# Feed-forward output product of a two-layer encoder: ten of eleven column groups as seven products of halves, and two of the seven placed between the norms

## The chip, the cores and the metric

The kernel runs on one core of one Trainium2 chip. The metric is the time of one execution on the device in microseconds; the time before is the median of three runs. TensorE is called PE below, VectorE DVE, ScalarE ACT, GpSimd POOL, and SyncE, which issues most of the DMA transfers, SP.

## The reference

Two layers on 512 tokens of 1024 features, in float32. Each layer has a feed-forward block, a token mixer, an attention into 256 memory tokens, and a second feed-forward block, each followed by a layer norm:

```python
def swiglu(x, w_gate, w_up, w_down):
    return (jax.nn.silu(x @ w_gate) * (x @ w_up)) @ w_down
...
#  x <- LN(alpha*x + 0.5*SwiGLU_1(x))
#  x <- LN(alpha*x + Mixer_i(x))
#  x <- LN(alpha*x + MemCrossAttn(x, mem))
#  x <- LN(alpha*x + 0.5*SwiGLU_2(x))
```

So there are four feed-forward blocks, called FFN0 to FFN3 below in order of time; the inner width is 2816 = 11 x 256. The mixer of the first layer follows FFN0, memory attention follows that, then FFN1, FFN2, the mixer of the second layer, memory attention again and FFN3, whose norm writes the output.

## The kernel before

**Tiles.** The 512 tokens are four tiles `x[0]` to `x[3]` of 128 tokens by 1024 features, kept in SBUF all the time (named `x0` to `x3` in the rows of an order). A transposed copy, in two parts `xh` and `xl`, feeds the projections. Every float32 product is three matmuls (`mm3`): each operand is split into a high and a low part, and high x high, high x low and low x high are accumulated in one PSUM bank. PSUM has eight banks, as three rings: three banks with the tag `a`, two with `d`, three with `t`. A bank of a ring is handed to the next tile of that tag when all users of the last one are done. SBUF work tiles come from a ring of 27 called `slab`, weights are loaded into a ring of two called `raw`.

**One feed-forward block (`ffn`).** The inner 2816 columns are eleven groups of 256. `hidden` computes a group: gate and up projections of two blocks of 128 columns (96 matmuls of 128x512), and `gated` multiplies. Then comes the output product, in two forms:

- `down_fast` takes two groups at once. The 512 tokens by 512 inner rows by 1024 outputs are cut in halves, so that the product is a 2x2 product of blocks, which is done with seven products of halves instead of eight. A product has two banks (b = 0, 1) with 6 matmuls each, so a pair of groups takes 84 matmuls. The sums and differences of halves that it needs are made on DVE (`mix`). The products are numbered as in the code and run in the order 1, 6, 2, 5, 7, 3, 4. Products 2, 3 and 4 go on in the banks of 1, 5 and 7 and add to them, so a bank is first added into `x` by DVE (the eviction), then gets the next product, and is evicted again to another place. Products 1 and 6 are evicted into `u2`, a slab that collects over all pairs of a block. `u2` is owed to six quarter tiles of `x`.
- `down` is the plain form: for each token tile and each half of the outputs one bank, three matmuls for each 128 inner rows, and an eviction into `x`.

Before, pairs 0 to 3 go through `down_fast`: columns 256g and 1024+256g. Then six additions on POOL put `u2` into `x` (tensor_tensor of 128x512, from SBUF to SBUF). Groups 8, 9 and 10 are plain: `down` for group 8, and one `down` for groups 9 and 10, which also does the layer norm of each token tile as soon as its two banks are evicted, and then (`to_features`) transposes it for the next stage, or writes it out in FFN3.

**The norm.** The last evictions give row sums as they go (`st`); DVE makes the negative mean `nmu`, ACT squares with a sum, POOL makes the reciprocal root `lny` in two small steps, and DVE does two passes over the 128x1024 tile (`scalar_tensor_tensor` with `ln_g`, then with `ln_b`).

**What sets the order.** All instructions are recorded by `Graph` and then emitted in one go, each engine's in the order that a greedy list scheduler finds: of what is ready by modelled costs, the one that stands first in the program. All instructions therefore carry line 140 (`op.call()`), and are told apart by the names of their tiles. On the chip each engine runs its queue in that order, and waits at an instruction whose operands or bank aren't ready.

Of the kernel before, what the change touches and what calls it, by code (L numbers as in the profile page):

```python
# [16 lines left out]
AF = mybir.ActivationFunctionType  # L17
ALU = mybir.AluOpType
AX = mybir.AxisListType

P = 128
D = 1024
S = 512
NT = S // P
# [225 lines left out]
class Kernel:  # L250
# [167 lines left out]
        v = self.x[t][:, h * 512 : (h + 1) * 512]  # L418
        self.nc.vector.scalar_tensor_tensor(out=v, in0=ps, scalar=coef, in1=v, op0=ALU.mult, op1=ALU.add)

    def down(self, acts, wts, coef, ln=None):

        nc = self.nc
        n = len(acts)
        for t in range(NT):
            st = self.small(2, "st") if ln else None
            for h in range(2):
                ps = self.ps("d")
                for i in range(n):
                    a = [z[:, t * P : (t + 1) * P] for z in acts[i]]  # L430
                    w = [z[:, h * 512 : (h + 1) * 512] for z in wts[i]]
                    self.mm3(ps, a, w, i == 0, i == n - 1)
                v = self.x[t][:, h * 512 : (h + 1) * 512]
                acc = {"accum_out": st[:, h : h + 1]} if ln else {}
                nc.vector.scalar_tensor_tensor(out=v, in0=ps, scalar=coef, in1=v, op0=ALU.mult, op1=ALU.add, **acc)
            if ln:
                self.layer_norm(t, st, ln["gb"])
                if ln["last"]:
                    dst = self.out.rearrange("(r c) d -> c r d", c=GRID_W)[16 * t : 16 * t + 16]
                    nc.sync.dma_start(out=dst, in_=self.x[t])  # L440
                else:
                    self.to_features(t)
# [59 lines left out]
        self.split(z, hi, lo)  # L502
        return hi, lo

    def down_fast(self, h1, h2, w, r1, r2, coef, u2):

        nc = self.nc
        a11, a21, a12, a22 = h1[:, 0], h1[:, 1], h2[:, 0], h2[:, 1]  # L510
        flat = lambda z: z.rearrange("p b n -> p (b n)")
        a11, a21, a12, a22 = map(flat, (a11, a21, a12, a22))

        def mix(dst, x, y, op):
            nc.vector.tensor_tensor(out=dst, in0=x, in1=y, op=op)
            return dst

        bs = {}
        for name, r, c in (("11", r1, 0), ("12", r1, 512), ("22", r2, 512), ("21", r2, 0)):
            z = self.slab(F32, (P, 2, 512))  # L520
            nc.sync.dma_start(out=z, in_=w[r : r + 256, c : c + 512].rearrange("(b p) f -> p b f", p=P))
            bs[name] = z

        def wide(z):
            got = self.slab(F32R, (P, 2, 512)), self.slab(F32R, (P, 2, 512))
            self.split(z, *got)
            return got

        left, right = {}, {}
        left[1] = self.split_pair(a11)  # L530
        right[1] = wide(bs["11"])
        t1 = mix(self.slab(F32, (P, 2, 512)), bs["12"], bs["11"], ALU.subtract)
        t2 = mix(self.slab(F32, (P, 2, 512)), bs["22"], t1, ALU.subtract)
        t3 = mix(bs["12"], bs["22"], bs["12"], ALU.subtract)
        s1 = mix(self.t2(F32), a21, a22, ALU.add)
        s2 = mix(self.t2(F32), s1, a11, ALU.subtract)
        left[6], right[6] = self.split_pair(s2), wide(t2)
        hh, hl = wide(h2.rearrange("p s b n -> p s (b n)"))
        left[2], left[4] = (hh[:, 0], hl[:, 0]), (hh[:, 1], hl[:, 1])
        right[2] = wide(bs["21"])  # L540
        t4 = mix(bs["21"], bs["21"], t2, ALU.subtract)
        left[5], right[5] = self.split_pair(s1), wide(t1)
        s3 = mix(self.t2(F32), a11, a21, ALU.subtract)
        left[7], right[7] = self.split_pair(s3), wide(t3)
        s4 = mix(self.t2(F32), a12, s2, ALU.subtract)
        left[3], right[3] = self.split_pair(s4), wide(bs["22"])
        right[4] = wide(t4)

        x = self.x
        n1, n2 = slice(0, 512), slice(512, 1024)  # L550
        first = u2 is None
        if first:
            u2 = self.slab(F32, (P, 2, 512))
        into = {
            1: lambda b: u2[:, b], 6: lambda b: u2[:, b], 2: lambda b: x[b][:, n1], 5: lambda b: x[2 + b][:, n2],
            7: lambda b: x[2 + b][:, n2], 3: lambda b: x[b][:, n2], 4: lambda b: x[2 + b][:, n1],
        }
        banks = {}
        for m, tag in ((1, "d"), (6, "t"), (2, 1), (5, "t"), (7, "d"), (3, 5), (4, 7)):
            for b in range(2):  # L560
                ps = banks[m, b] = self.ps(tag) if isinstance(tag, str) else banks[tag, b]
                for q in range(2):
                    st = [z[:, q * 256 + b * P : q * 256 + (b + 1) * P] for z in left[m]]
                    self.mm3(
                        ps, st, [z[:, q] for z in right[m]], isinstance(tag, str) and q == 0, q == 1, skip_group_check=True
                    )
                v = into[m](b)
                if m == 1 and first:
                    nc.scalar.activation(v, ps, AF.Copy, scale=coef)
                else:  # L570
                    nc.vector.scalar_tensor_tensor(out=v, in0=ps, scalar=coef, in1=v, op0=ALU.mult, op1=ALU.add)
        return u2

    def ffn(self, i, ln_i, last, aside=None):

        nc = self.nc
        wg, wu, wd = (self.a[n][i] for n in ("ffn_w_gate", "ffn_w_up", "ffn_w_down"))
        coef, u2 = 0.5 / ALPHA, None
        for g in range(4):
            h1, h2 = (self.slab(F32, (P, 2, 2, 256)) for _ in range(2))  # L580
            if g == 0:
                self.ffn_by_tokens(wg, wu, i == 0, h1)
            else:
                self.hidden(wg, wu, 256 * g, h1)
            self.hidden(wg, wu, 1024 + 256 * g, h2)
            u2 = self.down_fast(h1, h2, wd, 256 * g, 1024 + 256 * g, coef, u2)
            if g == 0 and aside:
                nc.after = [op for op in nc.ops if op.dma][-1], {"sync"}
                aside()
                nc.after = None  # L590
        for t, h in ((0, 1), (2, 0), (2, 1), (1, 1), (3, 0), (3, 1)):
            v = self.x[t][:, h * 512 : (h + 1) * 512]
            nc.gpsimd.tensor_tensor(out=v, in0=v, in1=u2[:, t % 2], op=ALU.add)
        acts, ws = [], []
        for g in range(8, 11):
            acts += [self.split_pair(z) for z in self.hidden(wg, wu, 256 * g)]
            if g == 9:
                continue
            rows = [8] if g == 8 else [9, 10]
            gb = self.load_ln(ln_i) if g == 10 else None  # L600
            ws = [z for r in rows for z in self.w_rows(wd, 256 * r)]
            self.down(acts, ws, coef, {"gb": gb, "last": last} if g == 10 else None)
            acts = []


    def transposed(self, parts):
# [583 lines left out]
    def run(self, phases=8):  # L1190
        nc, a = self.nc, self.a
        self.ident = self.tile(self.cst, [P, P], F32, "ident")
        make_identity(self.tc.nc, self.ident)
        self.xh = self.tile(self.big, [P, KB, S], F32R, "xh")
        self.xl = self.tile(self.big, [P, KB, S], F32R, "xl")
        self.x = []
        for t in range(NT):
            self.x.append(self.tile(self.big, [P, D], F32, f"x{t}"))
        self.nhalf = self.tile(self.cst, [P, 8], F32, "nhalf")
        nc.gpsimd.memset(self.nhalf, -0.5)  # L1200
        self.junk = self.tile(self.cst, [P, D], BF16, "junk")
        steps = [
            lambda last: self.ffn(0, 0, last, self.masks),
            lambda last: self.mixer_ab(1, last),
            lambda last: self.memory(0, 2, last),
            lambda last: self.ffn(1, 3, last, self.bias_tables),
            lambda last: self.ffn(2, 4, last),
            lambda last: self.mixer_c(5, last),
            lambda last: self.memory(1, 6, last),
            lambda last: self.ffn(3, 7, last),  # L1210
        ]
        for i in range(phases):
            steps[i](i == phases - 1)
        nc.emit()
# [72 lines left out]
```

## Time and profile before

| | |
|---|---|
| Time, median of three runs | 2249.1 us (2248.18 to 2251.29) |
| Profiled execution: its time / its span | 2250.06 us / 2248.3 us |
| PE busy | 2207.0 us, 98% of the span, 11312 matmuls |
| DVE busy | 1420.1 us, 63% |
| ACT busy | 882.7 us, 39% |
| POOL busy | 287.0 us, 13% |
| Mean granted clock of TensorE | 0.996 |
| DMA | 221.09 MB, 98 GB/s over the span |

The profile is of one execution; its time is the span and 1.8 us around it, and it lies 1.0 us above the median of the three runs. A row of a group gives the engine, the operation, the tile written and the tiles read, the count, busy time and mean duration, and the idle time of that engine just before. A row of the timeline gives the start and the duration in us. DVE's consecutive instructions overlap by some 0.08 us in these rows, and the matmuls of PE too, so that the pitch from start to start says more of PE than the duration of one.

### The profile page before, as it was taken

The numbers are of one execution on the slowest core, as the hardware profiler recorded it, in microseconds if no ns is written. First come the engines' busy times: TensorE is split into PE (matmuls) and PEld (weight loads), VectorE is DVE, ScalarE is ACT, GpSimd is POOL, SyncE is SP. The second block draws the span as 40 slices with busy tenths as digits, with TensorE's granted clock in tenths as the row PEclk, the third lists the DMA queues.
The fourth block names the chain that finished last, engine by engine and source line by source line (L and its number), as shares of the span: only waits on it lengthen the run. The fifth ranks groups of instructions, "written<-read, shape, count | busy, mean of one in ns | idle before, by whom it ended". The sixth has DMA issues, their size and how long they took to land. (4 is left out here: it accounts for less than half of the span.)

```text
span 2248.3 us, 28157 instructions
## 1 busy us (share of the span) xinstructions
PE 2207.0 (98%) x11312; PEld 1871.7 (83%) x11312; DVE 1420.1 (63%) x2116; ACT 882.7 (39%) x1418; POOL 287.0 (13%) x391
## 2 busy tenths in 40 slices
PE   8999999999999999999999999999999999999998
PEld 7888888778898888888888888888888988888886
DVE  5666646788745766665655667368776457666653
ACT  4323332566433433333333333256554434333331
POOL 0000203543000100001100003013411001000011
PEclk9999999999999999999999999999999999999999
DMA  6333241003333332225312334212233333322241
GB/s 207 129 120 113 67 154 57 20 20 90 124 106 113 113 113 90 72 83 168 105 40 86 113 117 150 75 62 68 69 113 96 129 113 113 113 82 72 85 137 38
DMA packets 168755, 221.09 MB, mean 98 GB/s; under 512 B 6192, under 2 KB 136880, under 8 KB 168624
## 3 DMA queue, kind: packets, MB, share of 16 engines
q1 hardware_dynamic: 165552, 208.80, 28.9%
q0 software_dynamic: 3072, 10.49, 1.3%
q8 instruction: 89, 1.46, 0.3%
q14 instruction: 42, 0.34, 0.1%
HBM read 217.17 MB, written 4.19 MB: 98 GB/s over the span
## 5 line engine op out<-in xcount | busy, mean ns | idle before, releaser
L140 PE MATMUL a<-xh,slab 128*128 128x512 f32 (+1 forms) x2960 | 890.8, 382 | 0.0
L140 PEld LDWEIGHTS a<-xh,slab 128*128 128x128 f32 x2960 | 549.1, 188 | 107.1
L140 PE MATMUL d<-slab,slab 128*128 128x512 f32 (+2 forms) x2432 | 572.5, 384 | 4.7 <-DVE slab L140 2.8
L140 PE MATMUL a<-xl,slab 128*128 128x512 f32 (+1 forms) x1480 | 565.0, 382 | 0.0
L140 PEld LDWEIGHTS d<-slab,slab 128*128 128x128 f32 x2432 | 441.1, 188 | 94.3 <-DVE slab L140 4.2
L140 ACT CAST slab<-raw 128x1024 fp32r<-128x1024 f32 x316 | 320.7, 1050 | 310.9 <-DMA raw<-ffn_w_gate 129.8
L140 DVE TENSOR_TENSOR slab<-raw,slab 128x1024 fp32r<-128x1024 f32 x316 | 391.6, 1254 | 72.9 <-ACT slab L140 55.4
L140 PEld LDWEIGHTS a<-xl,slab 128*128 128x128 f32 x1480 | 278.3, 188 | 53.0
L140 DVE TENSOR_TENSOR slab<-slab,slab 128x1024 fp32r<-128x1024 f32 (+2 forms) x208 | 241.4, 1184 | 18.9 <-ACT slab L140 17.6
L140 ACT CAST slab<-slab 128x1024 fp32r<-128x1024 f32 (+1 forms) x144 | 140.1, 1000 | 238.4 <-DVE slab L140 238.3
L140 ACT CAST slab<-t 128x512 fp32r<-128x512 f32 (+3 forms) x261 | 143.5, 572 | 225.9 <-DVE t L140 142.0
L140 PE MATMUL a<-slab,slab 128*128 128x256 f32 (+3 forms) x1336 | 204.9, 303 | 6.2 <-DVE slab L140 2.6
L140 DVE TENSOR_TENSOR slab<-a,t 128x512 f32<-128x512 f32 x56 | 38.7, 691 | 269.3 <-PE a L140 269.3
L140 PEld LDWEIGHTS a<-slab,slab 128*128 128x128 f32 x1336 | 180.6, 194 | 21.5 <-DVE slab L140 6.0
L140 DVE TENSOR_TENSOR slab<-t,slab 128x512 fp32r<-128x512 f32 (+3 forms) x261 | 164.3, 654 | 42.7 <-ACT slab L140 41.5
L140 DVE SCALAR_TENSOR_TENSOR x<-d,x 128x512 f32<-128x512 f32 x216 | 147.3, 685 | 48.3 <-PE d L140 47.3
L140 PE MATMUL t<-slab,slab 128*128 128x512 f32 (+1 forms) x648 | 152.1, 379 | 0.0
L140 ACT ACTIVATE t<-a 128x512 f32<-128x512 f32 (+2 forms) x104 | 57.4, 552 | 225.2 <-PE a L140 203.0
L140 POOL TENSOR_TENSOR x<-x,slab 128x512 f32<-128x512 f32 x24 | 46.0, 1950 | 780.7 <-DVE x L140 780.7
L140 PEld LDWEIGHTS t<-slab,slab 128*128 128x128 f32 x648 | 115.7, 188 | 25.0 <-DVE slab L140 2.2
L140 POOL TENSOR_TENSOR t<-t,l 128x256 f32<-128x256 f32 (+2 forms) x104 | 80.1, 785 | 308.4 <-DVE l L140 308.4
L140 PE MATMUL a<-slab,xh 128*128 128x256 f32 (+1 forms) x432 | 98.1, 319 | 4.1 <-ACT xh L140 4.0
(97 smaller groups left out, 1810.0 us busy)
## 6 DMA issues: line engine op xcount, KB each, us to landing
raw<-ffn_w_gate SPq DMA_DIRECT2D x40, 1024.0 KB
raw<-ffn_w_up SPq DMA_DIRECT2D x40, 1024.0 KB
slab<-ffn_w_down SPq DMA_DIRECT2D x64, 512.0 KB
raw<-ffn_w_down SPq DMA_DIRECT2D x12, 1024.0 KB
raw<-mem_w_kv SPq DMA_DIRECT2D x8, 1024.0 KB
raw<-mem_w_kv SPq DMA_DIRECT2D x16, 512.0 KB
raw<-mem_w_q SPq DMA_DIRECT2D x8, 1024.0 KB
raw<-mem_w_o SPq DMA_DIRECT2D x8, 1024.0 KB
```

Of the source, the lines that this page charges most:

```text
L140: op.call = lambda: fn(*args, **kw)
```

## The change

`ffn` now takes five pairs through `down_fast`: columns (0, 1024), (256, 1280), (512, 1536), (768, 1792) and (2048, 2304). Only the group at 2560 stays plain. The seven products run in the order 1, 6, 2, 5, 3 and then 7, 4; the last two are handed back as a function `rest`. In pairs 0 to 3 it is called at once. In pair 4 it is called after `down`, with its norms, has dealt with token tiles 0 and 1 (products 7 and 4 go only to tiles 2 and 3), and `down` of tiles 2 and 3 follows. The six additions on POOL now stand right behind product 6 of pair 4. `down`, which the mixers and the memory attention use as well, takes its banks from `d` for the first half of the outputs and from `a` for the second.

```diff
-    def down(self, acts, wts, coef, ln=None):
+    def down(self, acts, wts, coef, ln=None, blocks=range(NT)):
...
-        for t in range(NT):
+        for t in blocks:
...
-                ps = self.ps("d")
+                ps = self.ps("da"[h])
...
-        for m, tag in ((1, "d"), (6, "t"), (2, 1), (5, "t"), (7, "d"), (3, 5), (4, 7)):
...
+        def run(*steps):
+            for m, tag in steps:
...
+                if m == 6 and last:
+                    for t, n in ((0, n2), (1, n2), (2, n1), (2, n2), (3, n1), (3, n2)):
+                        nc.gpsimd.tensor_tensor(out=x[t][:, n], in0=x[t][:, n], in1=u2[:, t % 2], op=ALU.add)
+
+        run((1, "d"), (6, "t"), (2, 1), (5, "t"), (3, 5))
+        return u2, lambda: run((7, "d"), (4, 7))
...
-        for g in range(4):
+        for g, (c1, c2) in enumerate(((0, 1024), (256, 1280), (512, 1536), (768, 1792), (2048, 2304))):
...
-        for t, h in ((0, 1), (2, 0), (2, 1), (1, 1), (3, 0), (3, 1)):
-            v = self.x[t][:, h * 512 : (h + 1) * 512]
-            nc.gpsimd.tensor_tensor(out=v, in0=v, in1=u2[:, t % 2], op=ALU.add)
-        acts, ws = [], []
-        for g in range(8, 11):
...
-            self.down(acts, ws, coef, {"gb": gb, "last": last} if g == 10 else None)
-            acts = []
+        acts = [self.split_pair(z) for z in self.hidden(wg, wu, 2560)]
+        gb = self.load_ln(ln_i)
+        ws, ln = self.w_rows(wd, 2560), {"gb": gb, "last": last}
+        self.down(acts, ws, coef, ln, range(2))
+        rest()
+        self.down(acts, ws, coef, ln, range(2, NT))
```

The first place is POOL's queue at the additions of FFN3. `slab_2922_3003` is `u2` before, `slab_2979_3060` is `u2` after the change; `x0` to `x3` are the token tiles, and a row with x2 is two instructions. Before:

```order
L140 TENSOR_TENSOR x2_6_87<-x2_6_87,slab_2922_3003 128x512
L140 TENSOR_TENSOR x3_7_88<-x3_7_88,slab_2922_3003 128x512
L140 TENSOR_TENSOR x0_4_85<-x0_4_85,slab_2922_3003 128x512
L140 TENSOR_TENSOR x1_5_86<-x1_5_86,slab_2922_3003 128x512
L140 TENSOR_TENSOR x2_6_87<-x2_6_87,slab_2922_3003 128x512
L140 TENSOR_TENSOR x3_7_88<-x3_7_88,slab_2922_3003 128x512
L140 DMA slab_3217_3298<-ln_g 128x1024
L140 DMA slab_3218_3299<-ln_b 128x1024
```

And now:

```order
L140 DMA slab_3296_3377<-ln_g 128x1024
L140 TENSOR_TENSOR x0_4_85<-x0_4_85,slab_2979_3060 128x512
L140 TENSOR_TENSOR x2_6_87<-x2_6_87,slab_2979_3060 128x512 x2
L140 TENSOR_TENSOR x1_5_86<-x1_5_86,slab_2979_3060 128x512
L140 TENSOR_TENSOR x3_7_88<-x3_7_88,slab_2979_3060 128x512 x2
L140 DMA slab_3297_3378<-ln_b 128x1024
```

The six additions are the same in kind and number. They now go by the half of `u2` that they read: three with the first half (one for x0, two for x2), then three with the second. The load of `ln_g` has moved ahead of them, that of `ln_b` stays behind them.

The second place is DVE's queue from the evictions of product 6 to those of product 3, in the last `down_fast` of FFN3. In the rows a source `d_...` or `t_...` is a bank that is evicted: `slab<-t` is product 6 into `u2`, `x0<-d` and `x1<-d` product 2, `x2<-t` and `x3<-t` product 5, `x2<-d` and `x3<-d` product 7, `x0<-t` and `x1<-t` product 3. A row `slab<-raw,slab` makes the low part of weights. Before:

```order
L140 SCALAR_TENSOR_TENSOR slab_2922_3003<-t_3145_3226,slab_2922_3003 128x512
L140 SCALAR_TENSOR_TENSOR x0_4_85<-d_3142_3223,x0_4_85 128x512
L140 TENSOR_TENSOR slab_3152_3233<-raw_3150_3231,slab_3151_3232 128x1024
L140 SCALAR_TENSOR_TENSOR x1_5_86<-d_3143_3224,x1_5_86 128x512
L140 SCALAR_TENSOR_TENSOR x2_6_87<-t_3146_3227,x2_6_87 128x512
L140 TENSOR_TENSOR slab_3154_3235<-raw_3150_3231,slab_3153_3234 128x1024
L140 SCALAR_TENSOR_TENSOR x3_7_88<-t_3147_3228,x3_7_88 128x512
L140 SCALAR_TENSOR_TENSOR x2_6_87<-d_3148_3229,x2_6_87 128x512
L140 TENSOR_TENSOR slab_3157_3238<-raw_3155_3236,slab_3156_3237 128x1024
L140 SCALAR_TENSOR_TENSOR x3_7_88<-d_3149_3230,x3_7_88 128x512
L140 SCALAR_TENSOR_TENSOR x0_4_85<-t_3146_3227,x0_4_85 128x512
```

And now:

```order
L140 SCALAR_TENSOR_TENSOR slab_2979_3060<-t_3275_3356,slab_2979_3060 128x512
L140 SCALAR_TENSOR_TENSOR x0_4_85<-d_3272_3353,x0_4_85 128x512
L140 TENSOR_TENSOR slab_3280_3361<-raw_3278_3359,slab_3279_3360 128x1024
L140 SCALAR_TENSOR_TENSOR x1_5_86<-d_3273_3354,x1_5_86 128x512
L140 TENSOR_TENSOR slab_3282_3363<-raw_3278_3359,slab_3281_3362 128x1024
L140 TENSOR_TENSOR slab_3285_3366<-raw_3283_3364,slab_3284_3365 128x1024
L140 SCALAR_TENSOR_TENSOR x2_6_87<-t_3276_3357,x2_6_87 128x512
L140 TENSOR_TENSOR slab_3287_3368<-raw_3283_3364,slab_3286_3367 128x1024
L140 SCALAR_TENSOR_TENSOR x3_7_88<-t_3277_3358,x3_7_88 128x512
L140 SCALAR_TENSOR_TENSOR x0_4_85<-t_3276_3357,x0_4_85 128x512
L140 SCALAR_TENSOR_TENSOR x1_5_86<-t_3277_3358,x1_5_86 128x512
```

The evictions of product 7 have gone from this place, those of product 3 follow those of product 5, and one more row of weights stands ahead of product 5's first eviction. That eviction, into x2, now has to come after POOL's third addition, which writes the same half of x2; product 5's second eviction, into x3, after the sixth. Before, nothing of POOL stood ahead of either. On PE, 40 matmuls now stand from the rest of product 6 (its last four matmuls for each bank, in one run) up to the first bank of product 3 and 51 up to its second; they are those of products 2 and 5 and some of the last hidden group's projection.

The third place is the end of FFN3 on DVE: the norms of the first tiles. Here `x,st<-d` or `x,st<-a` is the last eviction of a half with its row sums, `nmu` the mean, `x<-x,nmu,slab` and `x<-x,lny,slab` the two passes of the norm. Before:

```order
L140 SCALAR_TENSOR_TENSOR x0_4_85,st_3229_3310<-d_3231_3312,x0_4_85 128x512
L140 TENSOR_SCALAR nmu_3232_3313<-st_3229_3310 128x1
L140 SCALAR_TENSOR_TENSOR x0_4_85<-x0_4_85,nmu_3232_3313,slab_3217_3298 128x1024
L140 SCALAR_TENSOR_TENSOR x1_5_86,st_3235_3316<-d_3236_3317,x1_5_86 128x512
L140 SCALAR_TENSOR_TENSOR x0_4_85<-x0_4_85,lny_3234_3315,slab_3218_3299 128x1024
L140 SCALAR_TENSOR_TENSOR x1_5_86,st_3235_3316<-d_3237_3318,x1_5_86 128x512
L140 TENSOR_SCALAR nmu_3238_3319<-st_3235_3316 128x1
L140 SCALAR_TENSOR_TENSOR x1_5_86<-x1_5_86,nmu_3238_3319,slab_3217_3298 128x1024
```

And now:

```order
L140 SCALAR_TENSOR_TENSOR x0_4_85,st_3303_3384<-a_3305_3386,x0_4_85 128x512
L140 SCALAR_TENSOR_TENSOR x1_5_86,st_3309_3390<-d_3310_3391,x1_5_86 128x512
L140 TENSOR_SCALAR nmu_3306_3387<-st_3303_3384 128x1
L140 SCALAR_TENSOR_TENSOR x1_5_86,st_3309_3390<-a_3311_3392,x1_5_86 128x512
L140 TENSOR_SCALAR nmu_3312_3393<-st_3309_3390 128x1
L140 SCALAR_TENSOR_TENSOR x0_4_85<-x0_4_85,nmu_3306_3387,slab_3296_3377 128x1024
L140 SCALAR_TENSOR_TENSOR x2_6_87<-d_3315_3396,x2_6_87 128x512
L140 SCALAR_TENSOR_TENSOR x0_4_85<-x0_4_85,lny_3308_3389,slab_3297_3378 128x1024
L140 SCALAR_TENSOR_TENSOR x1_5_86<-x1_5_86,nmu_3312_3393,slab_3296_3377 128x1024
L140 SCALAR_TENSOR_TENSOR x3_7_88<-d_3316_3397,x3_7_88 128x512
L140 SCALAR_TENSOR_TENSOR x1_5_86<-x1_5_86,lny_3314_3395,slab_3297_3378 128x1024
```

The banks of tile 1 are evicted before the passes of tile 0's norm, and the evictions of product 7 (into x2 and x3, from `d`) stand between the passes of the norms of tiles 0 and 1. On PE the same stretch holds 24 matmuls of `down` for tiles 0 and 1, 24 of products 7 and 4, and 24 of `down` for tiles 2 and 3, where before it held 96 of `down` for four tiles.

More of the change, by code (lines that the diff above doesn't have):

```diff
@@ L558, in down_fast @@
         banks = {}
-        for m, tag in ((1, "d"), (6, "t"), (2, 1), (5, "t"), (7, "d"), (3, 5), (4, 7)):
[L560 to L572, printed above, removed]
+        def run(*steps):
+            for m, tag in steps:
+                for b in range(2):
+                    ps = banks[m, b] = self.ps(tag) if isinstance(tag, str) else banks[tag, b]
+                    for q in range(2):
+                        st = [z[:, q * 256 + b * P : q * 256 + (b + 1) * P] for z in left[m]]
+                        self.mm3(
+                            ps, st, [z[:, q] for z in right[m]], isinstance(tag, str) and q == 0, q == 1, skip_group_check=True
+                        )
+                    v = into[m](b)
+                    if m == 1 and first:
+                        nc.scalar.activation(v, ps, AF.Copy, scale=coef)
+                    else:
+                        nc.vector.scalar_tensor_tensor(out=v, in0=ps, scalar=coef, in1=v, op0=ALU.mult, op1=ALU.add)
+                if m == 6 and last:
[3 more added lines that the diff above has]
+        return u2, lambda: run((7, "d"), (4, 7))
     def ffn(self, i, ln_i, last, aside=None):
@@ L583, in ffn @@
             else:
-                self.hidden(wg, wu, 256 * g, h1)
-            self.hidden(wg, wu, 1024 + 256 * g, h2)
-            u2 = self.down_fast(h1, h2, wd, 256 * g, 1024 + 256 * g, coef, u2)
+                self.hidden(wg, wu, c1, h1)
+            self.hidden(wg, wu, c2, h2)
+            u2, rest = self.down_fast(h1, h2, wd, c1, c2, coef, u2, g == 4)
+            if g < 4:
+                rest()
             if g == 0 and aside:
@@ L590, in ffn @@
                 nc.after = None
-        for t, h in ((0, 1), (2, 0), (2, 1), (1, 1), (3, 0), (3, 1)):
-            v = self.x[t][:, h * 512 : (h + 1) * 512]
-            nc.gpsimd.tensor_tensor(out=v, in0=v, in1=u2[:, t % 2], op=ALU.add)
-        acts, ws = [], []
-        for g in range(8, 11):
[L596 to L601, printed above, removed]
-            self.down(acts, ws, coef, {"gb": gb, "last": last} if g == 10 else None)
-            acts = []
+        acts = [self.split_pair(z) for z in self.hidden(wg, wu, 2560)]
+        gb = self.load_ln(ln_i)
+        ws, ln = self.w_rows(wd, 2560), {"gb": gb, "last": last}
+        self.down(acts, ws, coef, ln, range(2))
+        rest()
+        self.down(acts, ws, coef, ln, range(2, NT))
     def transposed(self, parts):
```

2 lines of the change are left out of this document (1 added, 1 removed).

## The prediction

> **What bounds the kernel now.** I read the page's busy times first, then the waits of PE, then the chain that ended last, and then the timeline of one feed-forward block. Busy times:
>
> ```profile
> PE 2207.0 (98%) x11312; PEld 1871.7 (83%) x11312; DVE 1420.1 (63%) x2116; ACT 882.7 (39%) x1418; POOL 287.0 (13%) x391
> ```
>
> PE works all the time. The view of its waits (what was waited for, total us, times, longest) adds up to 29.6 us in thirteen rows; the largest are the load of the input and the end of the norms:
>
> ```profile
> PE t L140 <- DMA x<-x: 6.9, 2, 5.8
> PE a L140 <- ACT xh L140: 4.0, 1, 4.0
> PE t L140 <- DVE x L140: 3.1, 4, 1.2
> PE d L140 <- DVE slab L140: 2.8, 8, 0.7
> ```
>
> No row names POOL's additions or an eviction as what holds a product. The chain of waits runs through long unbroken stretches of PE in FFN3, and gives the price of a 128x512 matmul: 43.29 us / 191 = 0.2266 us.
>
> ```profile
> 2014.21 43.29 PE a L140 x191
> ```
>
> So a matmul taken out of a feed-forward block is worth its full 0.2266 us, and a new wait of PE costs its full length. About 0.2%, 4.5 us, is what a measurement of this kernel can tell from no change. The profiled execution took 2250.06 us, 1.0 above the median of the runs; I make the sum as a difference and put it on the median.
>
> **Part 1: fewer matmuls.** A pair of groups takes 2 x 48 = 96 matmuls in the plain form and 84 as seven products. One more pair in each of four blocks: 4 x 12 x 0.2266 = **-10.9 us**, wholly on PE's path. The sums of halves, splits and evictions that the fifth pair brings to DVE lie beside PE as those of the first four do (DVE 63%); I put them at nothing. If that cover were gone, the row of 2.8 us above (eight waits for a slab of DVE, in all blocks) shows the size.
>
> **Part 2: the additions of POOL ahead of product 3.** Before, they ran when all of the pair was evicted and plain work followed. In the timeline of FFN3 (start, duration):
>
> ```profile
> 2133.78 11.52 POOL L140 TENSOR_TENSOR x<-x,slab 128x512 f32<-128x512 f32 x6 [243.39 <-DVE x L140]
> ```
>
> The four batches take 11.50 to 11.52 us; the tile's view has the spread of the 24 (min/median/max ns):
>
> ```profile
> L140 POOL TENSOR_TENSOR x<-x,slab x24: 1281/2238/2371, 265.3 to 2144.0; 128x512 f32<-128x512 f32 x24
> ```
>
> One alone takes 1.28 us. The others are long because they alternate with DVE's weight rows, which read two operands from SBUF and are drawn out too, from 1.21 us outside to 1.99 within, while evictions from PSUM keep their 0.68:
>
> ```profile
> 2128.72 1.21 DVE L140 TENSOR_TENSOR slab<-raw,slab 128x1024 fp32r<-128x1024 f32 x1
> ...
> 2135.72 0.69 DVE L140 SCALAR_TENSOR_TENSOR x<-t,x 128x512 f32<-128x512 f32 x1 [0.29 <-PE t L140]
> 2136.33 1.99 DVE L140 TENSOR_TENSOR slab<-raw,slab 128x1024 fp32r<-128x1024 f32 x1
> 2138.24 0.68 DVE L140 SCALAR_TENSOR_TENSOR x<-t,x 128x512 f32<-128x512 f32 x1
> ```
>
> The Trainium skill, "SBUF — State Buffer", section "Who interferes with whom", says that DVE and GpSimd share a pair of ports as an exclusive lock, which an instruction of DVE takes when both inputs are in SBUF and GpSimd reads there, and not with one input in SBUF. These rows agree (1.99 against 0.68 us). The rule speaks against an early place for the additions, where four such rows of DVE wait in the same stretch.
>
> Now the additions begin when product 6 is evicted, and who waits for them? Product 5's first eviction adds into the half of x2 that the third addition writes, its second into x3 behind the sixth. Product 3 goes on in product 5's banks, so PE's first matmul of its second bank stands behind the sixth addition. All of PE's queue stands behind that matmul: the last hidden group, with nothing to go around it. The times, in the numbers of FFN3 before:
>
> ```profile
> 2124.84 2.00 PE L140 MATMUL t<-slab,slab 128*128 128x512 f32 x8
> ...
> 2126.33 0.68 DVE L140 SCALAR_TENSOR_TENSOR slab<-t,slab 128x512 f32<-128x512 f32 x1
> ```
>
> The first row is the rest of product 6; the second its first eviction, which ends at 2127.01. In the new order of PE, product 3's second bank starts 51 matmuls behind the start of that first row: 2124.84 + 51 x 0.2266 = 2136.40. Evicted it is at 2127.01 + 0.08 (the gap from engine to engine) + 11.52 + 0.08 + 0.68 = 2139.4. So PE stands still for **3.0 us** in a block, part of it (about 1) ahead of the first bank, which the third addition holds: 4 x 3.0 = **+12.0 us**. Bounds: six additions of 1.28 take 7.7 us, and the wait is gone, 0; six of 2.37 take 14.2 us, 5.7 each, +22.8. I take 11.52, since the new stretch holds four weight rows of DVE like the old one.
>
> DVE stands in order behind its eviction too, so its weight rows and the next gating come late by the same 3 us; PE is late by then as well, and I add nothing.
>
> **Part 3: the ends of the blocks.** Behind the start of the last `down`, PE had 96 matmuls and has 72 now, 24 x 0.2266 = 5.4 us less to hide the norms under; DVE has four evictions (products 7 and 4) more among them, about 4 x 0.6 = 2.4 us. Before, PE and DVE were close there. The end of FFN2, ahead of the second mixer:
>
> ```profile
> 1445.10 11.50 PE L140 MATMUL d<-slab,slab 128*128 128x512 f32 x50
> ...
> 1474.02 1.29 DVE L140 SCALAR_TENSOR_TENSOR x<-x,lny,slab 128x1024 f32<-128x1024 f32 x1 [0.38 <-POOL lny L140]
> ...
> 1475.45 1.06 PE L140 MATMUL t<-ident,x 128*128 128x128 f32 x8 [0.50 <-DVE x L140]
> ```
>
> The last tile's norm ended 30.2 us behind the first `down` matmul and PE waited 0.50 for it. DVE's own work there (per tile two evictions, two passes of 1.2 and two splits of 0.6, with the small steps 5.4 us) can't be moved up by 5.4 us: counted through in the new order, tile 2's norm is done about 24 us behind the first `down` matmul, where PE has come through its 72 matmuls (16.3), the transposes of two tiles and half a projection at 21.4. So PE waits 2.8 for tile 2 and some 1.4 more for tile 3: **+4.2**. Ahead of the first mixer and of FFN2 more projection work lies ready: I take +1.0 and +1.5 for FFN0 and FFN1. In FFN3 nothing follows; the end was
>
> ```profile
> 2215.57 21.95 PE L140 MATMUL d<-slab,slab 128*128 128x512 f32 x96
> ...
> 2238.47 0.21 DVE L140 TENSOR_SCALAR nmu<-st 128x1 f32<-128x1 f32 x1
> ...
> 2242.06 1.28 DVE L140 SCALAR_TENSOR_TENSOR x<-x,lny,slab 128x1024 f32<-128x1024 f32 x1 [0.72 <-POOL lny L140]
> ```
>
> 5.8 us from PE's last matmul (2237.52) to the last pass's end. Now the last banks of tiles 2 and 3 end within 7 matmuls of each other, and tile 3's mean stands behind an eviction and a pass of tile 2, about 1.5 us later: **+1.5**. Together **+8.2**; bounds 0 (all covered) and 4 x 5.4 = 21.6 (DVE bound everywhere and no earlier than before).
>
> **Part 4: the clock.** TensorE's granted clock fell twice within the work (columns: length, PE, PEld, DVE, ACT, POOL, clock, DMA, GB/s):
>
> ```profile
> 590.00:594.00 4.00, 3.72 (x18) 3.72 (x19) 3.21 (x4) 0.00 (x0) 0.30 (x1) 0.57 0.80 255
> 1713.00:1720.00 7.00, 5.46 (x24) 5.11 (x24) 4.33 (x5) 1.35 (x3) 2.17 (x2) 0.53 0.45 150
> 573.40:577.00 3.60, 3.60 (x21) 3.06 (x20) 3.41 (x9) 2.55 (x5) 0.69 (x2) 1.00 0.00 0
> ...
> 590.28 4.28 PE L140 MATMUL a<-slab,slab 128*128 128x256 f32 x21 [1.24 <-DVE slab L140]
> ```
>
> An idle 1.24 us stood ahead of the first fall; the third window, behind another short idle, shows none. A fall of some 3.4 us at half clock costs 1.7 us. The new stops of 2 to 3 us, four in the pairs and one ahead of the mixer, could each do it: 0 to 5 x 1.7 = 8.5. I take two of the five: **+3.4**. The Trainium skill, "TensorE: Matmul & The Clock Gate", Part 1, has the clock at half after an idle window of about 3.4 us that runs free of the program; by it, stops of 2 to 3 us would not be a full window, the term would be 0 and the sum 2258.4.
>
> Moved `a` and `d` banks in mixers and memory leave PE's rows there nearly as they were; 0, with a bound of 1 us either way.
>
> **Sum:** -10.9 + 12.0 + 8.2 + 3.4 = +12.7, on the median 2249.1: **2261.8 us**.
>
> **Rivals.**
> B, faster: the additions don't hold product 3. If DVE's weight rows come mostly outside them (their raw weights or ACT's high parts come later), six additions take near 7.7 us, and the evictions end at 2135.5, ahead of 2136.40. It decides at a batch of about 8.5 us. Against it stands that each of four batches before took 11.5. Then -10.9 + 0 to 8.2: 2238 to 2246, about 2242. Chance 0.16.
> C, no difference: the additions hold PE as worked out, but the mixers' and projections' work covers the norms, and the clock stays, as in the window at 573.40: -10.9 + 12.0 + 0 to 2 = 2250 to 2252. For it: PE waited only 3.1 us in all for x at four ends before. Chance 0.17.
> D, much slower: every addition meets a weight row of DVE (2.37 each), and the clock falls at each stop: -10.9 + 22.8 + 8.2 + 8.5 = +28.6, 2278; halves of it 2268 to 2278. Chance 0.17.
> The forecast, 2254 to 2268, has 0.50. The clock by itself, 0 or 8.5, moves it within that.
>
> **Numbers.** The range leaves out most of B and the upper half of D, 0.2 together: 2244 to 2273. Faster by over 0.2% (under 2244.6) is most of B: 0.14. Within 0.2% are C and the edges of B and the forecast: 0.19. Slower: 0.67.
>
> **What would show it.** Right: PE's waits have a new row of t banks that wait for DVE's x, with eight or so waits and about 12 us; a batch of additions starts right behind product 6 and takes about 11.5 us; PE has 48 matmuls of 128x512 fewer (11264); PE's transposes ahead of the second mixer wait some 4 us for x. Wrong: batches of additions under 9 us and no such row (B); the row, but PE's transposes wait as little as before, with no new clock windows (C); batches of 14 us or clock windows of 0.5 in each block (D). A new wait of PE that comes from the evictions of products 7 and 4, which now stand between the norms, would make the working wrong in another way.

## The result, and the profile after

The changed kernel takes 2264.34 us (median of 4 runs, 2261.14 to 2265.6) against 2248.8 for the kernel before on the same chip: the medians are 15.5 us apart; 12.7 was forecast, on a range of 2244 to 2273. The ratio, which is estimated from the single runs and not from the two medians, is 1.0062, 95% interval 1.0051 to 1.0074, that is 11 to 17 us.

The busy times of the changed kernel, whose span is 2261.6 us:

```profile
PE 2203.0 (97%) x11264; PEld 1867.7 (83%) x11264; DVE 1486.7 (66%) x2192; ACT 901.5 (40%) x1438; POOL 296.5 (13%) x391
```

The 48 matmuls are gone (11264), and PE is busy 4 us less in a span that is 13.3 us longer. The view of PE's waits has a row of another size at its head (before: 3.1 us in 4 waits):

```profile
PE t L140 <- DVE x L140: 17.6, 16, 2.2
PE t L140 <- DMA x<-x: 7.0, 2, 5.9
PE a L140 <- DVE slab L140: 4.8, 3, 1.9
PE a L140 <- ACT xh L140: 4.3, 2, 4.0
PE a L140 <- ACT slab L140: 3.8, 2, 1.9
```

The place is seen in the timeline of FFN3's last pair: in turn POOL's additions, then rows of DVE, then rows of PE (start, duration, the operation, idle time before it and what ended that):

```profile
2201.12 11.91 POOL L140 TENSOR_TENSOR x<-x,slab 128x512 f32<-128x512 f32 x6 [3.31 <-DVE slab L140]
...
2200.35 0.68 DVE L140 SCALAR_TENSOR_TENSOR slab<-t,slab 128x512 f32<-128x512 f32 x1
2204.48 3.95 DVE L140 TENSOR_TENSOR slab<-raw,slab 128x1024 fp32r<-128x1024 f32 x2
2208.36 0.68 DVE L140 SCALAR_TENSOR_TENSOR x<-t,x 128x512 f32<-128x512 f32 x1
2208.96 1.69 DVE L140 TENSOR_TENSOR slab<-raw,slab 128x1024 fp32r<-128x1024 f32 x1
2213.06 1.29 DVE L140 SCALAR_TENSOR_TENSOR x<-t,x 128x512 f32<-128x512 f32 x2 [2.41 <-POOL x L140]
...
2209.18 1.62 PE L140 MATMUL t<-slab,slab 128*128 128x512 f32 x6 [1.06 <-DVE x L140]
2213.81 1.67 PE L140 MATMUL t<-slab,slab 128*128 128x512 f32 x6 [1.85 <-DVE x L140]
```

Product 6's first eviction ends at 2201.03, the additions start 0.09 us later and take 11.91 us. DVE waits 2.41 us for the sixth (product 5's second eviction), and PE starts product 3's second bank 0.75 us after that eviction began. The two stops are 2.9 us by these rows. FFN0 has the same two (1.04 and 1.86), FFN1 about the same, FFN2 one of 2.16. The row counts from the end of a matmul's 0.39 us; from start to start, less the pitch of 0.2266 us, the stops are 3.2, 3.2, 2.3 and 3.2 us in FFN0 to FFN3, 12.0 together.

The time by stage, from the views of windows: each window ends at the last transpose of the fourth token tile. The rows are FFN0 to the first memory attention, FFN1, FFN2 to the second memory attention, and FFN3 up to PE's last matmul (window, length, PE busy, then the other engines). Before, and after:

```profile
35.10:767.60 732.50, 723.13 (x3724) 609.90 (x3723) 482.12 (x809) 308.98 (x542) 129.63 (x180) 1.00 0.30 95
767.60:1122.80 355.20, 355.13 (x1674) 296.86 (x1673) 216.98 (x263) 120.04 (x153) 19.95 (x16) 1.00 0.31 101
1122.80:1893.20 770.40, 760.22 (x4162) 655.14 (x4161) 500.60 (x781) 328.79 (x569) 116.73 (x172) 1.00 0.30 98
1893.20:2237.10 343.90, 343.90 (x1584) 286.61 (x1583) 199.20 (x242) 106.60 (x134) 18.11 (x14) 1.00 0.26 86
```

```profile
35.60:774.90 739.30, 723.60 (x3718) 611.39 (x3716) 500.02 (x828) 313.50 (x547) 137.64 (x180) 0.99 0.30 94
774.90:1132.70 357.80, 354.70 (x1681) 296.64 (x1679) 232.22 (x281) 125.44 (x159) 20.68 (x16) 1.00 0.31 103
1132.70:1904.70 772.00, 758.19 (x4133) 652.38 (x4131) 517.81 (x800) 333.21 (x573) 117.60 (x172) 0.99 0.29 96
1904.70:2249.20 344.50, 341.50 (x1568) 283.67 (x1567) 213.23 (x257) 109.88 (x138) 16.30 (x12) 1.00 0.26 85
```

PE stood still in FFN1 for 0.07 us before (355.20 - 355.13) and for 3.1 us after, in FFN3 for 0 and 3.0. The first stage, 6.8 us longer, holds the most; one part of that is FFN0's stop, the others are taken apart below.

### The profile page after: what moved, and what is told of

Read it like the earlier page. It is cut to its first block, busy times and chain, and to the rows that moved or that the text cites. A ratio compares the mean times of both kernels' runs of the same rounds, so it can differ in the third digit from the quotient of the medians.

```text
span 2261.6 us, 28207 instructions
## 1 busy us (share of the span) xinstructions
PE 2203.0 (97%) x11264; PEld 1867.7 (83%) x11264; DVE 1486.7 (66%) x2192; ACT 901.5 (40%) x1438; POOL 296.5 (13%) x391
## 5 line engine op out<-in xcount | busy, mean ns | idle before, releaser
L140 PE MATMUL d<-slab,slab 128*128 128x512 f32 (+2 forms) x1856 | 451.5, 381 | 2.2 <-DVE slab L140 0.9
L140 DVE TENSOR_TENSOR slab<-raw,slab 128x1024 fp32r<-128x1024 f32 x300 | 374.8, 1264 | 56.3 <-ACT slab L140 56.0
L140 PEld LDWEIGHTS d<-slab,slab 128*128 128x128 f32 x1856 | 335.0, 188 | 66.4 <-DVE x L140 1.5
L140 DVE TENSOR_TENSOR slab<-slab,slab 128x1024 fp32r<-128x1024 f32 (+2 forms) x260 | 303.0, 1188 | 26.9 <-ACT slab L140 25.0
L140 PE MATMUL a<-slab,slab 128*128 128x256 f32 (+3 forms) x1720 | 301.4, 322 | 7.7 <-ACT slab L140 3.8
L140 ACT CAST slab<-slab 128x1024 fp32r<-128x1024 f32 (+1 forms) x180 | 175.3, 1000 | 310.3 <-DVE slab L140 307.4
L140 PEld LDWEIGHTS a<-slab,slab 128*128 128x128 f32 x1720 | 251.0, 191 | 37.1 <-DVE slab L140 6.3
L140 PE MATMUL t<-slab,slab 128*128 128x512 f32 (+1 forms) x792 | 191.0, 385 | 11.2 <-DVE x L140 10.8
L140 PEld LDWEIGHTS t<-slab,slab 128*128 128x128 f32 x792 | 143.1, 190 | 45.7 <-DVE x L140 7.1
L140 DVE SCALAR_TENSOR_TENSOR x<-d,x 128x512 f32<-128x512 f32 x168 | 114.8, 684 | 30.2 <-PE d L140 29.6
```

The lines of the kernel that those rows point to most:

```text
L140: op.call = lambda: fn(*args, **kw)
```

## The experiments

The profiled runs of one kernel differ by a few us with the clock, so the times are medians, each against the kernel before on the same chip (medians there 2248.8 to 2249.8). Where two changed kernels are compared, it is by their distances from the kernel before. The intervals of the ratios are some 2 us to either side with ten or eleven runs, 3 to 4 with four.

**Additions behind product 3.** The short edit:

```diff
-                if m == 6 and last:
+                if m == 3 and last:
```

> The six additions of a block now stand behind product 3 of the fifth pair instead of product 6, so that product 5's evictions wait for none of them; the rest is as in the changed kernel. Theory (the additions hold product 3): the waits of PE for x ahead of product 3 (3.2 us in FFN0, FFN1 and FFN3, 2.3 in FFN2, 12.0 in all) go, and with them two clock windows that follow such a wait (about 1.7 each): 2264.3 - 12.0 - 0 to 3.4 = 2249 to 2252. Rival (the stop only stands in for another one, as product 5's banks or DVE's queue, which come late anyway): the wait moves elsewhere and the time stays at 2260 to 2265.

2249.83 us, ratio 1.0001 (0.9991 to 1.001): the theory. POOL's additions now come in two parts, and PE goes from product 5 to the two banks of product 3 without a stop, in FFN3:

```profile
2195.02 3.99 POOL L140 TENSOR_TENSOR x<-x,slab 128x512 f32<-128x512 f32 x2 [3.31 <-DVE slab L140]
2199.54 7.52 POOL L140 TENSOR_TENSOR x<-x,slab 128x512 f32<-128x512 f32 x4
...
2197.07 2.43 PE L140 MATMUL t<-slab,slab 128*128 128x512 f32 x10
2199.57 1.52 PE L140 MATMUL t<-slab,slab 128*128 128x512 f32 x6
2201.38 1.52 PE L140 MATMUL t<-slab,slab 128*128 128x512 f32 x6
```

The early place of the additions costs 15.2 us (15.5 above the kernel before, against 0.4), and without it the kernel with five pairs is level with the one before. In this profile a stop of another kind stands in FFN0: 2.96 us ahead of tile 0's transposes. The profiled run is the slowest of the ten, 3.8 us above their median, and whether the others have this stop isn't on record. DVE's first pass waited for ACT's square, which stood behind casts of the mixer's weights, and these for a transfer:

```profile
357.68 2.00 ACT L140 CAST slab<-raw 128x1024 fp32r<-128x1024 f32 x2 [1.66 <-DMA raw<-ab_w_in]
359.58 1.15 ACT L140 ACTIVATE junk<-x,nmu 128x1024 bf16<-128x1024 f32 x1
...
364.21 1.37 PE L140 MATMUL t<-ident,x 128*128 128x128 f32 x8 [2.96 <-DVE x L140]
```

**The needed additions first.** Still behind product 6, but in another order:

```diff
-                    for t, n in ((0, n2), (1, n2), (2, n1), (2, n2), (3, n1), (3, n2)):
+                    for t, n in ((2, n2), (3, n2), (0, n2), (1, n2), (2, n1), (3, n1)):
```

> Of the six additions, still behind product 6, the two that product 5's evictions need come first in the program (x2, x3 second halves, then x0, x1, then the others). The scheduler puts x2's at the first place of POOL's queue and x3's at the fourth, after all three with the first half of u2. Theory (place in the batch sets the wait): the first bank of product 3 is no longer held (1.2 us less in three blocks), the second waits for four additions instead of six, about two thirds of 11.9 = 7.9 us, ahead of the deciding 8.6 us: wait near 0 to 1, so 2251 to 2256. Rival (it is the port that POOL and DVE alternate on, whatever the order, that makes DVE late): the wait stays near 3 us, 2262 to 2266.

2261.68 us, ratio 1.0057 (1.0042 to 1.0072): not the theory's 2251 to 2256, though not for the rival's reason. The fourth addition does end earlier, as was worked out: in FFN1 the batch starts at 1071.36 and product 5's second eviction at 1078.93, 7.6 us later.

```profile
1078.93 0.69 DVE L140 SCALAR_TENSOR_TENSOR x<-t,x 128x512 f32<-128x512 f32 x1 [2.40 <-POOL x L140]
...
1079.68 0.50 PE L140 MATMUL t<-slab,slab 128*128 128x512 f32 x1 [1.78 <-DVE x L140]
```

But the scheduler, which has its own cost for an addition (512 x 2.17 + 110 = 1221 ns; the measured ones take 2 us in the mean), saw the eviction come early too, and put product 3's second bank 38 matmuls behind the rest of product 6 instead of 51. So 13 matmuls of cover, 2.9 us, went, against evictions 4.4 us earlier, and a stop of 1.8 us is left in each block where there were 2.9 (2.2 in FFN2). This profile also has the stop ahead of tile 0's transposes in FFN0, 3.00 us, which the changed kernel doesn't have; it takes back most of what the shorter stops win. What I had missed is that the order of PE is no constant of such an edit.

**Products 7 and 4 ahead of all norms.**

```diff
-        self.down(acts, ws, coef, ln, range(2))
         rest()
-        self.down(acts, ws, coef, ln, range(2, NT))
+        self.down(acts, ws, coef, ln)
```

> Products 7 and 4 of the fifth pair go ahead of the last down with its norms, instead of between the norms of tiles 1 and 2. Theory (the ends are short of PE work to hide norms under, DVE bound): behind tile 0's banks PE has 36 matmuls instead of about 60, 5.4 us less cover, so more waits for x at the three ends with a following stage and a later last pass in FFN3: 4 to 5.4 us at two or three of the ends, 2272 to 2282. Rival (the order of these products does not matter, projection work of the next stage covers the norms): 2262 to 2267.

2264.0 us, ratio 1.0066 (1.0051 to 1.0081): the rival. The place of the two products "behind the norms of the first" is worth nothing over the kernel. From the traces this is no absence of effects: with the stages bounded as above, it is 4.9 us shorter from FFN0 to the memory attention, 2.3 longer in FFN1 and 1.3 longer in FFN3 with its tail. Of the 4.9, some 3.4 us are the clock: that stage has one stretch of 3.4 us at half clock in this run, and three in the profile of the changed kernel.

**Banks d alone in `down`.**

```diff
-                ps = self.ps("da"[h])
+                ps = self.ps("d")
```

> down takes both banks of a token tile from the two-deep ring d again, as before the change, in the blocks, mixers and memory attention. Theory (the banks are no term of the difference): within 2 us of the changed kernel, 2262 to 2267. Rival (with products 7 and 4 on d as well, two banks for everything at the ends make PE wait for evictions): 2267 to 2275.

2272.58 us, ratio 1.0107 (1.009 to 1.0124): the rival, 7.6 us slower than the changed kernel (8.2 by the two medians). A row of PE's waits shows 4.1 us of it, a bank of `d` that waits for DVE to evict it; before has no such row, and in the changed kernel it has 0.2 us:

```profile
PE d L140 <- DVE x L140: 4.1, 8, 1.2
```

**Late additions, products 7 and 4 first in FFN0 alone.** An `if i == 0` around the two orders of the end.

> Additions behind product 3, and in FFN0 alone products 7 and 4 ahead of the last down. In the run with the additions behind product 3 PE stood 3.1 us ahead of the transposes of tile 0 in FFN0, since ACT's square for the norm stood behind two casts of the mixer's weights, whose transfer came late. Theory (the end of FFN0 is held by ACT behind that transfer, and work of PE and DVE that stands ahead of the norms covers it): the run with products 7 and 4 first was 4.9 us shorter from FFN0 to the memory attention, so 2249.8 - 3 to 5 = 2245 to 2247. Rival (what is won in FFN0 goes into the mixer's own waits for these weights): 2249 to 2251.

2249.36 us, ratio 0.9999 (0.999 to 1.0008): the rival. FFN0's end has no stop of 2.96 us any more, but PE waits in the mixer instead, 0.75 and 2.66 us for POOL (the changed kernel has one such wait, of 1.33 us):

```profile
418.70 1.97 PE L140 MATMUL t<-ident,slab 128*128 128x128 f32 x8 [2.66 <-POOL slab L140]
```

**Late additions, products 7 and 4 first in all blocks.** The edits of the first and third experiment together.

> Additions behind product 3, products 7 and 4 ahead of the last down in all four blocks. Theory (the two changes are independent; the order of the products is worth nothing over the four blocks, as 2264.0 against 2264.3 with early additions says): 2248 to 2251. Rival (with the additions late and products 7 and 4 early, product 7's and 4's evictions into tiles 2 and 3 and the six additions meet, and the norms of tiles 0 and 1 come late): 2254 to 2262.

2253.16 us, ratio 1.0013 (1.0004 to 1.0022), between the two expectations: the edits aren't quite independent. With late additions, products 7 and 4 early cost some 3 us over the program.

**No additions.** The changed kernel without the six lines; `u2` is never put into `x`.

> The changed kernel without the six additions of a block: u2 is never put into x, so that part of the output product is left out. Theory (the additions cost only by holding product 3, and cost nothing behind it): as with the additions behind product 3, 2247 to 2251. Rival (even there they cost, by the port that they share with DVE's weight rows): 2240 to 2245.

2247.82 us, ratio 0.999 (0.9981 to 0.9999): the theory, barely. By the distances from the kernel before, the additions cost 17.6 us ahead of product 3, and 2.4 behind it, which the intervals hardly tell from nothing. This kernel is also the one that shows what the rest of the change does without them (the fifth pair, the place of products 7 and 4, the banks): 10.9 us less matmuls, 2.0 us less time. Its windows, in the stages as above:

```profile
35.70:768.80 733.10, 719.68 (x3716) 608.67 (x3715) 496.88 (x828) 313.31 (x547) 124.05 (x174) 1.00 0.29 95
768.80:1123.20 354.40, 354.14 (x1681) 296.80 (x1679) 230.00 (x281) 125.67 (x159) 9.99 (x10) 1.00 0.32 104
1123.20:1893.20 770.00, 758.67 (x4134) 653.45 (x4132) 515.37 (x800) 333.38 (x573) 106.68 (x166) 0.99 0.29 96
1893.20:2234.00 340.80, 340.80 (x1568) 283.76 (x1567) 211.03 (x257) 109.91 (x138) 4.41 (x6) 1.00 0.26 86
```

Each stage would be 2.7 us shorter by its matmuls. Against before they are 0.6 longer, 0.8, 0.4 and 3.1 shorter; the tail behind the last matmul is 1.1 longer (span 2246.3 - 2234.0 = 12.3 against 2248.3 - 2237.1 = 11.2). So 3.3, 1.9, 2.3 and 0.7 us were given back, stage by stage; each stage also holds what the new banks change there and its falls of the clock.

**The kernel before with banks d and a.** The one line of the fourth experiment, in the other direction.

> The kernel before with one edit of the change alone: down takes its second half's bank from ring a. Theory (in the kernel before the two banks of ring d were enough, PE had no stop in a down; the 8.2 us that the banks are worth in the changed kernel come from products 7 and 4 on ring d among the norms): 2247 to 2251. Rival (ring a helps the mixers and memory attention too): 2240 to 2246.

2247.38 us, ratio 0.9989 (0.998 to 0.9999): at the edge of the theory. The banks are worth about 2.5 us there, at the edge of the interval, and 7.6 in the changed kernel. In the trace the second mixer is 1.8 us shorter, where it has one stretch at half clock for two before (1.7 us), so what the banks do by themselves isn't settled. Its windows, in the stages as above:

```profile
36.60:770.60 734.00, 723.62 (x3730) 612.54 (x3728) 482.84 (x809) 309.09 (x542) 132.87 (x180) 1.00 0.30 95
770.60:1124.70 354.10, 354.02 (x1670) 296.67 (x1669) 216.70 (x263) 119.86 (x153) 19.94 (x16) 1.00 0.31 101
1124.70:1892.90 768.20, 759.56 (x4166) 654.92 (x4165) 500.47 (x781) 328.65 (x569) 115.87 (x172) 1.00 0.30 98
1892.90:2236.10 343.20, 343.20 (x1581) 286.25 (x1579) 199.00 (x242) 106.79 (x134) 18.12 (x14) 1.00 0.26 86
```

**The kernel before with early additions.** Of the change, only this:

```diff
-        for m, tag in ((1, "d"), (6, "t"), (2, 1), (5, "t"), (7, "d"), (3, 5), (4, 7)):
+        for m, tag in ((1, "d"), (6, "t"), (2, 1), (5, "t"), (3, 5), (7, "d"), (4, 7)):
...
+            if m == 6 and last:
+                for t, n in ((0, n2), (1, n2), (2, n1), (2, n2), (3, n1), (3, n2)):
+                    nc.gpsimd.tensor_tensor(out=x[t][:, n], in0=x[t][:, n], in1=u2[:, t % 2], op=ALU.add)
```

> The kernel before with the additions alone moved behind product 6 of the fourth pair, and product 3 ahead of 7 in the program (the scheduler puts product 7's first matmuls ahead of 3 again in part; product 3's second bank stands 52 matmuls behind the rest of product 6). Theory (the additions hold product 3 through product 5's evictions): a new wait of some 3 us in each of four blocks, +12, and 0 to 3 for the clock: 2260 to 2265. Rival (the stop needs the fifth pair or products 7 and 4 put off, as without product 7 in between): 2249 to 2253.

2267.96 us, ratio 1.0079 (1.0064 to 1.0095): 18.6 us slower, the theory and some 3 us above it. The stops are at the same place, in FFN3 0.60, 0.28 and 1.52 us by the rows, 2.9 from start to start:

```profile
2147.66 1.61 PE L140 MATMUL t<-slab,slab 128*128 128x512 f32 x6 [0.60 <-DVE x L140]
2149.79 0.98 PE L140 MATMUL d<-slab,slab 128*128 128x512 f32 x3 [0.28 <-DVE x L140]
2152.29 1.10 PE L140 MATMUL t<-slab,slab 128*128 128x512 f32 x3 [1.52 <-DVE x L140]
```

So the wait needs neither the fifth pair nor products 7 and 4 put off. With product 3 ahead of 7, as here and in the changed kernel, it is a matter of the additions' place. Early additions with product 7 still ahead of 3 weren't run.

**Five pairs in two blocks.** The changed kernel with late additions, in FFN1 and FFN3 only (a tuple `five` of blocks; the others have the four pairs and three plain groups of before), and its counterpart in FFN0 and FFN2:

```diff
+        five = i in (1, 3)
+        pairs = [(256 * g, 1024 + 256 * g) for g in range(4)] + [(2048, 2304)] * five
```

> Five pairs, with the additions behind product 3 and products 7 and 4 among the norms, in FFN1 and FFN3 only, which a feed-forward block and nothing follow; FFN0 and FFN2, which a mixer follows, in the form of before; down takes banks d and a everywhere. Theory (what the 48 matmuls save is lost at the ends of FFN0 and FFN2, where the norms meet the mixer's first weights on ACT and DVE): two blocks with 5.4 us less PE work keep most of it, less about 1.3 in FFN3's tail, and the banks give 2.5 more as they did in the kernel before: 2243 to 2246. Rival (every end loses alike, about 2.2 a block): 2246 to 2249.

> The counterpart: five pairs with late additions in FFN0 and FFN2 only, FFN1 and FFN3 in the form of before; down takes banks d and a everywhere. Theory (the ends ahead of the mixers lose what is saved): 5.4 us saved, 6 to 8 lost, 2.5 from the banks: 2247 to 2251. Rival (every end loses alike): 2246 to 2249.

FFN1 and FFN3: 2243.77 us, ratio 0.9976 (0.9967 to 0.9985), as the theory has it and faster than both kernels. FFN0 and FFN2: 2253.0, ratio 1.0017 (1.0008 to 1.0026), slower even than the theory's 2247 to 2251. Both save the same number of matmuls, and they are 9.2 us apart. Seen from the kernel before with the same banks (2.5 us under the kernel before), two blocks win 3.1 of 5.4 us, and the two that a mixer follows lose 6.2 beside the 5.4 that they save. The two sum to +3.1, and all four blocks (the first experiment) stand at +2.8. That every end loses alike is out. Part of the loss is the clock: the profile of FFN0 and FFN2 has eight stretches of 3.4 us at half clock, that of FFN1 and FFN3 two, though the former is of the slowest of its ten runs.

## Why the prediction was right

**Part 1** holds: 48 matmuls fewer, and PE's long stretches keep their pitch.

**Part 2** was the term that decides, and it was right in mechanism, place and size. The batches take 11.9 us (11.52 was taken); the stops of PE are 3.2, 3.2, 2.3 and 3.2 us from start to start, against 3.0 each, and 12.0 together as forecast. Leaving the additions out takes 17.6 us off, moving them behind product 3 15.2, and moving them and product 3 forward in the old kernel puts 18.6 on. All are more than 12.0. In the profiles, the kernel without additions is 15.3 us shorter: 12.0 of stops, and 1.7 of one stretch at half clock less. The old kernel with early additions is 17.3 longer: 11.6 of stops and 3.4 of two such stretches. The remaining 1.6 and 2.3 us stay open.

**Part 3** met its sum, in part by luck: the stages gave back 3.3, 1.9, 2.3 and 0.7 us, 8.2 together, where I had 1.0, 1.5, 4.2 and 1.5 for the ends. But the new banks are in these numbers too. I had put them at nothing, with a bound of 1 us either way; they are worth some 2.5 us in the kernel before and 7.6 in the changed one. Against the kernel before with the new banks, the same windows give back 1.8, 3.0, 4.5 and 1.5 us, 10.8 together, and the two profiles differ by two stretches at half clock besides. So the share of each end isn't settled. By the medians the sum is -10.9 of matmuls, -2.5 of banks (if that small difference is theirs), +17.6 of additions and +11.3 at the ends, the last two with their share of the clock: the banks, put at nothing, hide a part of what the ends and the additions cost beyond the forecast.

What is clear is that the ends ahead of the mixers were taken too low: 5.2 us, where the last pair of experiments, with late additions, has 11.6 (5.4 and 6.2); for FFN1 and FFN3, 3.0 stands against 2.3. I had sized FFN0's from the projection work that lies ready ahead of the first mixer. In each profile that has the fifth pair in FFN0, products 7 and 4 among the norms and the new banks, a projection there waits for the low part of its weights, a row of 1.97 us on DVE behind the mixer's first small steps:

```profile
398.72 0.50 PE L140 MATMUL a<-slab,xh 128*128 128x512 f32 x1 [1.94 <-DVE slab L140]
```

That the ends ahead of the mixers are the costly ones is shown by the last pair of experiments; that it is the weights is only read from this row and from ACT's casts in the first experiment, and the one try to mend it (the fifth experiment) moved the wait on. The end of FFN2 showed its wait nearly as worked out (2.8 and 1.4 for tiles 2 and 3; 24 less 21.4 is 2.6):

```profile
1483.49 1.06 PE L140 MATMUL t<-ident,x 128*128 128x128 f32 x8 [2.06 <-DVE x L140]
1486.42 1.94 PE L140 MATMUL t<-ident,x 128*128 128x128 f32 x8 [1.12 <-DVE x L140]
```

In FFN3 the time from the start of the last matmul to the last pass's end went from 6.2 to 7.35 us (2249.24 to 2256.59), 1.1 where I had 1.5.

**Part 4**, two falls of the clock, was a little low. Of the windows (length, the engines, and the granted clock third from the end), two of the four places with new stops are followed by a fall, FFN0 and FFN2; FFN1 and FFN3 aren't. The second and fourth windows are these falls, the first and third the 3.4 us ahead of them; the last two hold FFN1's second stop:

```profile
332.10:335.50 3.40, 1.54 (x7) 0.95 (x6) 1.29 (x2) 1.74 (x2) 2.11 (x3) 1.00 0.85 275
335.50:338.90 3.40, 3.40 (x9) 2.62 (x8) 2.31 (x3) 0.00 (x0) 1.19 (x2) 0.50 1.09 329
1434.60:1438.00 3.40, 1.24 (x7) 0.73 (x5) 3.23 (x3) 0.21 (x1) 3.40 (x2) 1.00 0.71 289
1438.00:1441.40 3.40, 3.40 (x8) 2.65 (x9) 1.21 (x2) 2.05 (x3) 2.28 (x4) 0.50 0.87 277
1079.60:1083.00 3.40, 2.59 (x11) 1.77 (x10) 1.28 (x1) 1.42 (x2) 3.40 (x3) 1.00 0.54 180
1083.00:1086.40 3.40, 2.36 (x10) 1.98 (x11) 1.96 (x4) 1.62 (x2) 0.78 (x2) 1.00 1.09 384
...
1437.98 2.44 PE L140 MATMUL t<-slab,slab 128*128 128x512 f32 x5 [2.16 <-DVE x L140]
```

In the 3.4 us of a fall 8 or 9 matmuls of 128x512 ran, where 15 would at full clock. By the rule that I had cited of the Trainium skill ("TensorE: Matmul & The Clock Gate", Part 1), a stop shorter than a window of 3.4 us would cost nothing. Here a single stop of 2.16 us was followed by a fall, so the measurement decides against that reading; the fall's length of 3.4 us is the length that the page gives for its window. In the profiled execution the whole program has six such windows where before it has three, about 5 us for 3.4 forecast; the falls differ from run to run, and the four runs of the changed kernel go with their mean clock, from 2261.14 us at 0.995 to 2265.6 at 0.992.

Rival B needed a batch of under 8.5 us and got 11.9. C needed the ends to be covered and the clock to stay; neither held. D's additions of 2.37 us each did not come (2.0 on the mean).

## What to carry to other kernels

A step that only has to be done "some time" is not free because its engine is idle: ask which later write to the same tile stands behind it, and what bank that write holds. Here six additions on an engine that is 87% idle cost 17.6 us at one place and about 2 at the next, a few lines on. And work taken off a bound engine is worth its length only where something else doesn't end at the same place; of the same saving of 5.4 us, two blocks kept about 3, and the two others ended some 6 us slower than without it, so try a change like this stage by stage, not all over.

## What was not expected of the hardware

The clock of TensorE fell right behind stops of 1.0 and 1.9 us (FFN0) and of 2.16 us (FFN2), well short of the 3.4 us that a fall then lasts, and did not fall behind the same stops of 1.0 and 1.9 us in FFN1 and FFN3.

The times of the falls show what differs. In the profile of the changed kernel they begin at 335.51, 495.94, 598.34, 1438.01, 1485.80 and 1728.15 us, and the distances are 47, 30, 246, 14 and 71 times 3.413 us: they lie on a grid of 3.413 us. FFN0's longer stop (1.86 us) and FFN2's (2.16 us) lie within the one step of that grid that ended where the fall began. In FFN1 a point of the grid, at 1083.03, cuts the stop of 1.85 us into 0.83 and 1.01; in FFN3 another, at 2212.84, cuts it into 0.88 and 0.97, and the clock stayed.

The other twelve profiles agree, from the loading of the input on to PE's last matmul. A step at full clock with 1.92 us or more without a matmul was always followed by one at half clock, a step at full clock with under 1.63 us never, and between the two both occur. So which of some equal stops costs 1.7 us more depends on where it lies on the grid, and the grid starts elsewhere in each of these profiles (a fall begins at 335.51 here, at 364.88 in the first experiment).
